# Hybrid attention layer on one core: the last merge's blocks and differences formed in PSUM, output products in another order, softmax sums by a one-operand operation

## The chip, the cores and the metric

The kernel runs on one core of one Trainium2 chip. The core has five queues of work: TensorE (PE in the profile; its weight loads are PEld), VectorE (DVE), ScalarE (ACT), GpSimd (POOL) and SyncE (SP), whose queue here only issues DMA transfers. Two on-chip memories matter: SBUF, from which the matmuls read, and PSUM, eight banks of 128 x 512 floats, into which they write. The metric is the device time of one execution in microseconds (us); lower is better.

## What is computed

One layer over 1024 latent tokens of width 1024, with a prefix of 256 context tokens. An input projection feeds three branches (neighbourhood attention, a short gated convolution, a Conformer convolution); their results are projected, weighted by sigmoid gates and added to m, which goes through one more projection. The parts that the change touches:

```python
def neighbourhood_attention(q, k, v, kc, vc, rpb):
    ...
        s = jnp.concatenate([s_loc.reshape(bsz, n_h, n_cb, Q_COLS, n_loc), s_ctx], axis=-1)
        p = jax.nn.softmax(s, axis=-1).astype(v.dtype)
    ...

def merge_branches(z, ya, yb, yc, w_out_a, w_out_b, w_out_c, w_o):
    ga, gb, gc = jnp.split(jax.nn.sigmoid(z[..., GATES:]), N_BRANCH, axis=-1)
    m = ga * (ya @ w_out_a) + gb * (yb @ w_out_b) + gc * (yc @ w_out_c)
    return m @ w_o

def hybrid_layer(x, xc, c, c_ctx, lp, update_ctx):
    ...
    x = x + gate * merge_branches(z, ya, yb, yc, lp['w_out_a'], lp['w_out_b'], lp['w_out_c'], lp['w_o'])
```

## The kernel before

**Numbers.** All of it is float32. A matrix that goes into a matmul is split in two parts of reduced precision: hi is a cast of it (ACT, L698 in `split`), lo is what the cast leaves (L699, a subtraction on DVE or POOL). Each product is then three matmuls: hi x hi, hi x lo, lo x hi (`mm3`, `product`).

**The attention** (`attend`, `scores`). For two blocks of 128 queries, the scores against context keys (`sc`) and against nearby keys (`sl`) are formed in PSUM; ACT takes the exponentials, and its accumulator gives one sum for the context keys and one for the nearby keys, per block. L571 adds them, L572 takes the reciprocals, L574 multiplies the exponentials; then PE transposes these (L581).

**The merges** (`merge`). m is held transposed: 8 tiles `mt[dm]` of 128 features x 1024 tokens. A merge goes over dm = 0 to 7 and over two halves b of 512 tokens; each half is 12 matmuls into one PSUM bank (`ops`), then L1089 multiplies it by the gates `gs`, loaded from memory, and L1090 adds it to `mt[dm]`. Three merges run one after the other, one per branch: branch 1 first (it writes `mt`, L1087), then branch 0, then branch 2, called the last merge here. In branch 0 L1090 of the first half runs on POOL. Beside branch 0 stand the steps of the Conformer's layer norm (`norm_steps`), which make `ych` and `ycl`, the inputs of the last merge, out of `zcin` (L1178 to L1182 and a split).

**The output product** uses a scheme with seven products for a 2 x 2 block matrix in place of eight. With M11 and M12 the two token halves of dm 0 to 3, and M21 and M22 those of dm 4 to 7, it needs seven right-hand sides, each of four tiles of 128 x 512: M11, M21, M22, MT1 = M12 - M11, MT2 = M22 - MT1, MT3 = M22 - M12 and MT4 = M21 - MT2. Before the change `merge` itself makes M11, MT1 and M21 (`part`); `m_sums(j)` makes the rest behind the merge, from `mt` and three sums `mraw`, all in SBUF. The weights' sums s1 to s4 are made on POOL (`w_sum`, L1257) from rows of w_o that DMA loads into three buffers (`wrf`), and split.

The output has four pairs n of 128-row blocks. `fin_first(n)` computes three products per pair: a1 x M11 into a bank `fa`, which ACT copies to p1 (L1281), s1 x MT1 into `fc`, and then a12 x M21 on top of `fa`; `put` (L1270) multiplies by the residual's gate, adds x and stores by DMA. `fin_rest(n)` has the four others: s2 x MT2 (`ff`), s4 x M22 (`fe`), s3 x MT3 (`fd`), and a22 x MT4 on top of `fd`. L1304 and L1307 combine `ff` with p1 and v.

**What sets the order.** The code names operations in program order; a scheduler then sets the order on each queue by a modelled timeline, and each queue keeps that order. Tile pools set reuse: `ps_x` has six PSUM banks, shared by `ops` and all banks of the output product; `ps_l` has two; `tmp` has six buffers in SBUF. A bank or buffer is written again only after its last reader. `issue_after` keeps `m_sums` behind the copy of p1.

Of the kernel before, what the change touches and what calls it, by code (L numbers as in the profile page):

```python
# [17 lines left out]
P = 128  # L18
# [27 lines left out]
def tile_hybrid(ctx: ExitStack, tc, x, xT, cx, cond, crow, ng, w_ada, b_ada, wqkv, wz,  # L46
# [437 lines left out]
    with tc.tile_pool(name="at", bufs=1, reuse_waits="tile") as at, \  # L484
# [63 lines left out]
        def scores(b0, qd, ql, ks, kc, bias):  # L548
# [8 lines left out]
            for i in range(2):  # L557
# [10 lines left out]
                act.activation(pc, sc[:, i], AF.Exp, bias=mn[:, 2 + i : 3 + i], scale=-1.0, accum_out=mn[:, 4 + i : 5 + i])  # L568
                act.activation(pl, pl, AF.Exp, bias=mn[:, 2 + i : 3 + i], scale=-1.0, accum_out=mn[:, 6 + i : 7 + i])
                pts.append((pt, n))  # L570
            dve.tensor_tensor(out=mn[:, 0:2], in0=mn[:, 4:6], in1=mn[:, 6:8], op=ALU.add)  # L571
# [494 lines left out]
    M11, M21, M22, MT1, MT2, MT3, MT4 = ([None] * 4 for _ in range(7))  # L1066
# [9 lines left out]
    def merge(br, ys, beside=lambda dm, b: None):  # L1076
        for dm in range(KT):
            w = w_merge(br, dm)
            gs = loaded(gd[br * KT + dm], "gs")
            if br == 1:  # L1080
                mt[dm] = of("mt", "mt", F32)
            for b in range(2):
                sl = B512[b]
                ps = ps_x.tile([P, 512], F32, tag="x", name="ops")
                mm3(ps, [(w[k][0], w[k][1], ys[k][0][:, sl], ys[k][1][:, sl]) for k in range(4)])
                if br == 1:
                    dve.tensor_tensor(out=mt[dm][:, sl], in0=ps, in1=gs[:, sl], op=ALU.mult)  # L1087
                else:
                    dve.tensor_tensor(out=gs[:, sl], in0=ps, in1=gs[:, sl], op=ALU.mult)  # L1089
                    (pool if br == 0 and b == 0 else dve).tensor_tensor(out=mt[dm][:, sl], in0=mt[dm][:, sl], in1=gs[:, sl], op=ALU.add)  # L1090
                beside(dm, b)
            if br == 2:
                first, second = halves(mt[dm])
                if dm < 4:
                    part(M11, dm, "ya0", first)
                    sub(dve, first, second, first)
                    part(MT1, dm, "ya1", first)
                else:
                    part(M21, dm - 4, "cv", first)
# [136 lines left out]
    def m_sums(j):  # L1236
        with tc.issue_after(state["fin"].ins):
            t1, b12 = halves(mt[j])
            b21, b22 = halves(mt[4 + j])
            raw = [tmp("mraw") for _ in range(3)]  # L1240
            sub(dve, raw[0], b22, t1)
            sub(dve, raw[1], b22, b12)
            sub(dve, raw[2], b21, raw[0])
            for blocks, t, r in ((MT2, t2, raw[0]), (MT3, t3, raw[1])):
                blocks[j] = t[j]
                split(*t[j], r, dve)
            for blocks, tag, r in ((M22, j, b22), (MT4, 4 + j, raw[2])):
                blocks[j] = halves(hp_pool.tile([P, S], F32R, tag=f"ha{tag}", name="mb"))
                split(*blocks[j], r, dve)
# [43 lines left out]
    def fin_rest(n):  # L1293
# [6 lines left out]
        s2 = w_sum("s2", s1, a11, ALU.subtract)  # L1300
        f = fin_bank("ff")
        product(f, wsplit(s2, pool), MT2, True, True)
        for t in (v, p1):
            dve.tensor_tensor(out=t, in0=f, in1=t, op=ALU.add)  # L1304
        for i, (x_, b, t) in enumerate(((x0, 1, v), (x1, 1, v), (x1, 0, p1))):
            dm = 2 * n + (i > 0)
            dve.scalar_tensor_tensor(out=x_[:, B512[b]], in0=t, scalar=gate[:, dm : dm + 1], in1=x_[:, B512[b]], op0=ALU.mult, op1=ALU.add)  # L1307
        s4 = w_sum("s4", a12, s2, ALU.subtract)
        e = fin_bank("fe")
        product(e, wsplit(s4, dve), M22, True, True)  # L1310
        put(2 * n, 1, e, x0[:, B512[1]])
# [3 lines left out]
        put(2 * n + 1, 1, d, x1[:, B512[1]])  # L1315
        product(d, wsplit(a22, dve), MT4, False, True)
        put(2 * n + 1, 0, d, x1[:, B512[0]])

    t2, t3 = ([halves(of("yb", "mb")) for _ in range(4)] for _ in range(2))
# [3 lines left out]
    for j, ns in enumerate(((0, 1), (2,), (2, 3), (3,))):  # L1323
        m_sums(j)
# [88 lines left out]
```

## Time and profile before

| what | value |
|---|---|
| median of 3 runs | 1121.64 us (1121.34 to 1122.14) |
| profiled execution, its own time | 1122.98 us |
| its span, first to last instruction | 1121.2 us |
| mean granted TensorE clock | 0.989 |
| PE busy 0 to 100 us | 81.24 us |
| PE busy 1000 to 1050 us | 50.00 us |
| PE busy 1050 to 1122 us | 60.83 us |

Times inside the execution are microseconds from the start of the span. A row of a timeline gives start, duration, engine, line, operation, output<-inputs by the program's names and shapes; in brackets the idle time of the engine before it and who ended that. A group of instructions gives count, busy time and mean duration in ns of one, then idle time before them. A stretch of the span gives, behind its length, the busy time and the number of instructions for PE, PEld, DVE, ACT and POOL, then PE's granted clock, the share of DMA and GB/s. PE's durations overlap, since matmuls are pipelined: its pace is read from starts.

### The profile page before, as it was taken

To read this page: it belongs to the slowest core of one execution; us is meant where nothing else is said; L and a number is where in the kernel's file an instruction comes from. 1 tells how busy PE (TensorE), PEld (TensorE's weight loads), DVE (VectorE), ACT (ScalarE), POOL (GpSimd) and SP (SyncE) were. 2 spreads that over 40 slices of the span, in tenths; PEclk is the share of its full clock that TensorE was granted. 3 is DMA by queue.
4 is the path that set the end of the run, shared out by engine and by line. 5 is a ranking of instruction groups with operands and counts; after the bars stand their busy time and mean duration, and the time that the engine had idled before them with its cause. 6 is when DMAs were issued, how large, how long until landed. Compare 5 with 4: busy or idle time off the path is not lost. (4 is left out here: it accounts for less than half of the span.)

```text
span 1121.2 us, 15882 instructions
## 1 busy us (share of the span) xinstructions
PE 1084.2 (97%) x5330; PEld 923.2 (82%) x5330; DVE 832.6 (74%) x1368; ACT 519.8 (46%) x1108; POOL 653.8 (58%) x643
## 2 busy tenths in 40 slices
PE   6889999999999999999999999999999999999998
PEld 5768898998998888887888888888888788878766
DVE  6983478666765655557995997897992479879995
ACT  6764576567556554445233232323434434533430
POOL 2254957437636951104958586868777562783860
PEclk7999999999999999999999999999999999999999
DMA  9555414313312332218133424343436996462443
GB/s 351 203 190 190 122 44 120 94 57 93 118 54 85 122 120 70 67 49 326 38 132 104 151 85 160 103 153 139 129 134 237 408 327 222 140 215 66 126 155 122
DMA packets 79458, 163.17 MB, mean 146 GB/s; under 512 B 10289, under 2 KB 31153, under 8 KB 79281
## 3 DMA queue, kind: packets, MB, share of 16 engines
q1 hardware_dynamic: 74768, 160.06, 41.5%
q10 hardware_dynamic: 4608, 2.10, 0.6%
q8 instruction: 42, 0.69, 0.3%
q14 instruction: 40, 0.32, 0.1%
HBM read 120.18 MB, written 44.50 MB: 147 GB/s over the span
## 5 line engine op out<-in xcount | busy, mean ns | idle before, releaser
L751 DVE SCALAR_TENSOR_TENSOR cv<-upad,cf_t,cv 128x512 f32<-128x512 f32 x240 | 166.8, 744 | 0.1
L699 POOL TENSOR_TENSOR wl<-s,wh 128x512 fp32r<-128x512 f32 x69 | 98.4, 1439 | 21.8 <-ACT wh L698 8.1
L90 POOL TENSOR_TENSOR wl<-wr,wh 128x384 fp32r<-128x384 f32 (+1 forms) x57 | 57.3, 1012 | 68.2 <-ACT wh L88 57.6
L698 ACT CAST wh<-s 128x512 fp32r<-128x512 f32 x92 | 55.9, 616 | 87.6 <-POOL s L702 66.0
L584 DVE TENSOR_TENSOR plo<-pp,phi 128x256 fp32r<-128x256 f32 (+2 forms) x96 | 54.5, 576 | 34.8 <-ACT phi L583 34.4
L541 POOL TENSOR_TENSOR bias<-mk,img 64x96 f32<-64x96 bf16 (+1 forms) x96 | 43.7, 462 | 36.9 <-DVE mn L567 20.5
L699 POOL TENSOR_TENSOR wl<-wr,wh 128x512 fp32r<-128x512 f32 x44 | 60.5, 1375 | 4.2 <-ACT wh L698 4.2
L775 PE MATMUL ga<-ha,wh 128*128 128x512 f32 x152 | 59.3, 390 | 1.2 <-ACT wh L698 1.2
L777 PE MATMUL ga<-ha,wl 128*128 128x512 f32 x152 | 59.2, 390 | 0.0
L776 PE MATMUL ga<-ha,wh 128*128 128x512 f32 x152 | 59.2, 390 | 0.0
L583 ACT CAST phi<-pp 128x256 fp32r<-128x256 f32 (+2 forms) x96 | 46.5, 494 | 26.6 <-PE pp L581 25.9
L567 DVE CUSTOM_DVE_ANT_0 pt<-sl,bias,mn 128x384 f32<-128x384 f32 (+1 forms) x64 | 37.2, 581 | 23.0 <-PE sl L564 21.7
L88 ACT CAST wh<-wr 128x384 fp32r<-128x384 f32 (+1 forms) x66 | 31.6, 487 | 39.8 <-PE zaps L108 14.3
L568 ACT ACTIVATE pt<-sc,mn 128x256 f32<-128x256 f32 x64 | 30.4, 475 | 40.1 <-DVE mn L567 40.0
L581 PE MATMUL pp<-ident,pt 128*128 128x128 f32 x304 | 47.0, 273 | 1.6 <-DVE pt L574 1.6
L803 POOL TENSOR_TENSOR s<-wr 128x512 f32<-128x512 f32 x16 | 23.8, 1486 | 38.7 <-DMA wr<-in_wz 38.6
L581 PEld LDWEIGHTS pp<-ident,pt 128*128 128x128 f32 x304 | 37.4, 140 | 9.0 <-ACT phi L583 1.3
L79 POOL TENSOR_TENSOR ssh<-ssh,half_neg 128x4 f32<-128x4 f32 (+1 forms) x40 | 41.4, 1036 | 2.9
L574 DVE TENSOR_SCALAR pt<-pt,mn 128x640 f32<-128x640 f32 (+1 forms) x64 | 41.6, 692 | 0.9
L78 POOL TENSOR_SCALAR ssh<-ssh 128x4 f32<-128x4 f32 (+1 forms) x40 | 10.5, 261 | 53.1 <-DVE ssh L227 49.4
L964 ACT ACTIVATE c<-c 128x512 f32<-128x512 f32 x18 | 11.4, 633 | 63.6 <-DVE c L781 48.0
L109 PE MATMUL ps<-wh,hb 128*128 128x384 f32 x112 | 39.3, 354 | 1.2 <-DVE hb L353 1.1
(421 smaller groups left out, 3896.8 us busy)
## 6 DMA issues: line engine op xcount, KB each, us to landing
wr<-in_wz SPq DMA_DIRECT2D x34, 512.0 KB, 4.0
gs<-gd SPq DMA_DIRECT2D x24, 512.0 KB, 5.0
wada<-in_w_ada SPq DMA_DIRECT2D x16, 512.0 KB, 8.7
wrf<-in_wo SPq DMA_DIRECT2D x16, 512.0 KB, 3.6
wr<-in_wz SPq DMA_DIRECT2D x36, 192.0 KB, 2.4
cht<-chd SPq DMA_DIRECT2D x24, 256.0 KB, 3.1
wro<-in_wout SPq DMA_DIRECT2D x24, 256.0 KB, 5.2
gd<-gate SPq DMA_DIRECT2D x22, 256.0 KB, 4.2
```

Source lines behind the costliest of these rows:

```text
L90: lo_eng.tensor_tensor(out=lo[:, :n], in0=raw[:, :n], in1=hi[:, :n].bitcast(F32), op=ALU.subtract)
L541: pool.tensor_tensor(out=dst, in0=mv, in1=iv, op=ALU.subtract)
L574: dve.tensor_scalar(out=pt[:, SPAN - n :], in0=pt[:, SPAN - n :], scalar1=mn[:, i : i + 1], scalar2=0.5, op0=ALU.mult, op1=ALU.mult)
L581: pe.transpose(out=pp[:, c * P : c * P + P], in_=src, identity=ident)
L583: act.copy(hi, v)
L584: dve.tensor_tensor(out=lo, in0=v, in1=hi.bitcast(F32), op=ALU.subtract)
L698: act.copy(hi, src)
L699: eng.tensor_tensor(out=lo, in0=src, in1=hi.bitcast(F32), op=ALU.subtract)
L751: dve.scalar_tensor_tensor(out=acc[b], in0=src, scalar=cf_t[:, i, j : j + 1], in1=acc[b], op0=ALU.mult, op1=ALU.add)
L775: pe.matmul(ps, wh, bh, start=first and j == 0, stop=False, skip_group_check=True)
L776: pe.matmul(ps, wh, bl, start=False, stop=False, skip_group_check=True)
L777: pe.matmul(ps, wl, bh, start=False, stop=last and j == 3, skip_group_check=True)
```

## The change

Three edits. The line numbers of the new program are up to 23 higher than those of the old behind the merge.

1. In `scores` the four sums of one step are laid out in pairs, and one `tensor_reduce` over pairs takes the place of the addition of two tensors.
2. In `merge`, L1089 writes its product back into the PSUM bank, and L1090 adds `mt` to it: into `mt` in branch 0, where all of these are now DVE's, and into the bank in the last merge. A new function `blocks` then makes from the banks M11, M21, M22 and MT1 with their splits, and the differences MT2, MT3 and MT4 unsplit (MT2 and MT3 in the two halves of `mt[j]`, MT4 in `t4`); ACT copies a block to SBUF where it is needed as the second operand. `m_sums` gives way to `m_splits`, in which ACT copies each of MT2, MT3 and MT4 into a bank of `ps_l`, from which it is split.
3. In `fin_rest` the product with M22 (`corner`) goes first for pairs 0 to 2; for pair 3 it goes between the two products into `fd`. The sums of `ff` with v and p1 go to PSUM (`fg`, and `ff` itself) and not over p1 and v.

```diff
@@ -565,10 +565,10 @@
                 pt = at.tile([P, SPAN + L], F32, tag="pt", name="pt", bufs=4)
                 pl, pc = pt[:, SPAN - n : SPAN], pt[:, SPAN:]
                 dve.tensor_tensor_reduce(pl, sl[:, :n], bias[:, o : o + n], 1.0, mn[:, i : i + 1], ALU.add, ALU.min, mn[:, 2 + i : 3 + i])
-                act.activation(pc, sc[:, i], AF.Exp, bias=mn[:, 2 + i : 3 + i], scale=-1.0, accum_out=mn[:, 4 + i : 5 + i])
-                act.activation(pl, pl, AF.Exp, bias=mn[:, 2 + i : 3 + i], scale=-1.0, accum_out=mn[:, 6 + i : 7 + i])
+                act.activation(pc, sc[:, i], AF.Exp, bias=mn[:, 2 + i : 3 + i], scale=-1.0, accum_out=mn[:, 4 + 2 * i : 5 + 2 * i])
+                act.activation(pl, pl, AF.Exp, bias=mn[:, 2 + i : 3 + i], scale=-1.0, accum_out=mn[:, 5 + 2 * i : 6 + 2 * i])
                 pts.append((pt, n))
-            dve.tensor_tensor(out=mn[:, 0:2], in0=mn[:, 4:6], in1=mn[:, 6:8], op=ALU.add)
+            dve.tensor_reduce(out=mn[:, 0:2], in_=mn[:, 4:8].rearrange("p (i a) -> p i a", a=2), axis=AX.X, op=ALU.add)
             dve.reciprocal(out=mn[:, 0:2], in_=mn[:, 0:2])
             for i, (pt, n) in enumerate(pts):
                 dve.tensor_scalar(out=pt[:, SPAN - n :], in0=pt[:, SPAN - n :], scalar1=mn[:, i : i + 1], scalar2=0.5, op0=ALU.mult, op1=ALU.mult)
@@ -1063,7 +1063,7 @@
 
 
     mt = [None] * KT
-    M11, M21, M22, MT1, MT2, MT3, MT4 = ([None] * 4 for _ in range(7))
+    M11, M21, M22, MT1, MT2, MT3, MT4, t4 = ([None] * 4 for _ in range(8))
 
     def halves(t):
         return t[:, :512], t[:, 512:]
@@ -1086,17 +1086,38 @@
                 if br == 1:
                     dve.tensor_tensor(out=mt[dm][:, sl], in0=ps, in1=gs[:, sl], op=ALU.mult)
                 else:
-                    dve.tensor_tensor(out=gs[:, sl], in0=ps, in1=gs[:, sl], op=ALU.mult)
-                    (pool if br == 0 and b == 0 else dve).tensor_tensor(out=mt[dm][:, sl], in0=mt[dm][:, sl], in1=gs[:, sl], op=ALU.add)
+                    dve.tensor_tensor(out=ps, in0=ps, in1=gs[:, sl], op=ALU.mult)
+                    dve.tensor_tensor(out=mt[dm][:, sl] if br == 0 else ps, in0=ps, in1=mt[dm][:, sl], op=ALU.add)
+                    if br == 2:
+                        blocks(dm, b, ps)
                 beside(dm, b)
-            if br == 2:
-                first, second = halves(mt[dm])
-                if dm < 4:
-                    part(M11, dm, "ya0", first)
-                    sub(dve, first, second, first)
-                    part(MT1, dm, "ya1", first)
-                else:
-                    part(M21, dm - 4, "cv", first)
+
+    first_half = {}
+
+    def blocks(dm, b, ps):
+
+        j = dm % 4
+        t1, m12 = halves(mt[j])
+        if b == 0:
+            first_half[dm] = ps
+            part((M11, M21)[dm // 4], j, ("ya0", "cv")[dm // 4], ps)
+            if dm < 4:
+                act.copy(t1, ps)
+            return
+        ps0 = first_half[dm]
+        if dm < 4:
+            act.copy(m12, ps)
+            sub(dve, ps0, ps, t1)
+            part(MT1, j, "ya1", ps0)
+            act.copy(t1, ps0)
+        else:
+            M22[j] = halves(hp_pool.tile([P, S], F32R, tag=f"ha{dm}", name="mb"))
+            split(*M22[j], ps, dve)
+            sub(dve, m12, ps, m12)
+            sub(dve, ps, ps, t1)
+            act.copy(t1, ps)
+            t4[j] = tmp("t4")
+            sub(dve, t4[j], ps0, t1)
 
 
 
@@ -1233,20 +1254,14 @@
     merge(2, yc_s)
 
 
-    def m_sums(j):
+    def m_splits(j):
         with tc.issue_after(state["fin"].ins):
-            t1, b12 = halves(mt[j])
-            b21, b22 = halves(mt[4 + j])
-            raw = [tmp("mraw") for _ in range(3)]
-            sub(dve, raw[0], b22, t1)
-            sub(dve, raw[1], b22, b12)
-            sub(dve, raw[2], b21, raw[0])
-            for blocks, t, r in ((MT2, t2, raw[0]), (MT3, t3, raw[1])):
-                blocks[j] = t[j]
-                split(*t[j], r, dve)
-            for blocks, tag, r in ((M22, j, b22), (MT4, 4 + j, raw[2])):
-                blocks[j] = halves(hp_pool.tile([P, S], F32R, tag=f"ha{tag}", name="mb"))
-                split(*blocks[j], r, dve)
+            t2, t3 = halves(mt[j])
+            for blk, src in ((MT2, t2), (MT3, t3), (MT4, t4[j])):
+                blk[j] = halves(hp_pool.tile([P, S], F32R, tag=f"ha{j}", name="mb") if blk is MT4 else of("yb", "mb"))
+                ps = ps_l.tile([P, 512], F32, tag="l", name="copy")
+                act.copy(ps, src)
+                split(*blk[j], ps, dve)
 
     def fin_bank(name):
         return ps_x.tile([P, 512], F32, tag="x", name=name)
@@ -1298,30 +1313,38 @@
         nc.sync.dma_start(x1, xT[2 * n + 1])
         s1 = w_sum("s1", a21, a22, ALU.add)
         s2 = w_sum("s2", s1, a11, ALU.subtract)
+        s4 = w_sum("s4", a12, s2, ALU.subtract)
+
+        def corner():
+            e = fin_bank("fe")
+            product(e, wsplit(s4, dve), M22, True, True)
+            return e
+
+        e = corner() if n < 3 else None
         f = fin_bank("ff")
         product(f, wsplit(s2, pool), MT2, True, True)
-        for t in (v, p1):
-            dve.tensor_tensor(out=t, in0=f, in1=t, op=ALU.add)
-        for i, (x_, b, t) in enumerate(((x0, 1, v), (x1, 1, v), (x1, 0, p1))):
+        g = fin_bank("fg")
+        dve.tensor_tensor(out=g, in0=f, in1=v, op=ALU.add)
+        dve.tensor_tensor(out=f, in0=f, in1=p1, op=ALU.add)
+        for i, (x_, b, t) in enumerate(((x0, 1, g), (x1, 1, g), (x1, 0, f))):
             dm = 2 * n + (i > 0)
             dve.scalar_tensor_tensor(out=x_[:, B512[b]], in0=t, scalar=gate[:, dm : dm + 1], in1=x_[:, B512[b]], op0=ALU.mult, op1=ALU.add)
-        s4 = w_sum("s4", a12, s2, ALU.subtract)
-        e = fin_bank("fe")
-        product(e, wsplit(s4, dve), M22, True, True)
-        put(2 * n, 1, e, x0[:, B512[1]])
+        if e is not None:
+            put(2 * n, 1, e, x0[:, B512[1]])
         s3 = w_sum("s3", a11, a21, ALU.subtract)
         d = fin_bank("fd")
         product(d, wsplit(s3, pool), MT3, True, True)
         put(2 * n + 1, 1, d, x1[:, B512[1]])
+        if e is None:
+            put(2 * n, 1, corner(), x0[:, B512[1]])
         product(d, wsplit(a22, dve), MT4, False, True)
         put(2 * n + 1, 0, d, x1[:, B512[0]])
 
-    t2, t3 = ([halves(of("yb", "mb")) for _ in range(4)] for _ in range(2))
     firsts = [fin_first(n) for n in range(4)]
     for n in (0, 1):
         next(firsts[n])
     for j, ns in enumerate(((0, 1), (2,), (2, 3), (3,))):
-        m_sums(j)
+        m_splits(j)
         for n in ns:
             next(firsts[n], None)
     for n in range(4):
```

The first place is on DVE, at the start of the last merge, where L1090 of its first half stands (`ops` are the PSUM banks, `gs` the gates, `mb` the lo parts of a block). Before:

```order
L1089 TENSOR_TENSOR gs<-ops,gs 128x512 x2
L1090 TENSOR_TENSOR mt<-mt,gs 128x512
L699 TENSOR_TENSOR mb<-mt,mb 128x512
L1089 TENSOR_TENSOR gs<-ops,gs 128x512
L1090 TENSOR_TENSOR mt<-mt,gs 128x512
```

and now:

```order
L1089 TENSOR_TENSOR ops<-ops,gs 128x512 x2
L1090 TENSOR_TENSOR ops<-ops,mt 128x512 x2
L1089 TENSOR_TENSOR ops<-ops,gs 128x512
L699 TENSOR_TENSOR mb<-ops,mb 128x512
L1090 TENSOR_TENSOR ops<-ops,mt 128x512
L699 TENSOR_TENSOR mb<-ops,mb 128x512
L1089 TENSOR_TENSOR ops<-ops,gs 128x512
L702 TENSOR_TENSOR ops<-ops,mt 128x512
```

Every operation now has a bank among its inputs, and a first difference (L702) stands in the middle of the merge; it is the ninth operation from the second L1089 on.

The second place is on ACT, behind the merge, around the copy of the fourth pair's `fa` to p1 (`pv`), on which a product of PE waits (`wh` are casts of weights or of their sums, s2 and s4; `mraw`, `copy` and `t4` belong to the differences). Before:

```order
L698 CAST mb_10509<-mraw_10722 128x512
L698 CAST mb_10513<-mraw_10723 128x512
L698 CAST mb_10732<-mt_9683 128x512
L698 CAST wh_10913<-wrf_10837 128x512
L698 CAST mb_10672<-mraw_10661 128x512
L698 CAST wh_10945<-s2_10942 128x512
L1281 COPY pv_10776<-fa_10759 128x512
```

and now:

```order
L1263 COPY copy_10757<-mt_9358 128x512
L1263 COPY copy_10762<-mt_9358 128x512
L698 CAST mb_10756<-copy_10757 128x512
L698 CAST mb_10761<-copy_10762 128x512
L698 CAST wh_10946<-wrf_10869 128x512
L1263 COPY copy_10767<-t4_10502 128x512
L698 CAST mb_10766<-copy_10767 128x512
L698 CAST wh_10980<-s4_10977 128x512
L1296 COPY pv_10809<-fa_10792 128x512
```

The copy for p1 stood behind a cast of the second pair's s2, and stands now behind one of its s4, which POOL makes two sums later; the casts of `mraw` are casts of banks, each behind a copy.

The third place is on PE, at the end of the last pair's product with MT3, into `fd`. Before:

```order
L775 MATMUL fd_11184<-mb_10514,wh_11185 128x512
L776 MATMUL fd_11184<-mb_10514,wh_11185 128x512
L777 MATMUL fd_11184<-mb_10514,wl_11186 128x512
L775 MATMUL fd_11184<-mb_10622,wh_11204 128x512
L776 MATMUL fd_11184<-mb_10622,wh_11204 128x512
```

and now:

```order
L775 MATMUL fd_11200<-mb_10840,wh_11201 128x512
L776 MATMUL fd_11200<-mb_10840,wh_11201 128x512
L777 MATMUL fd_11200<-mb_10840,wl_11202 128x512
L775 MATMUL fe_11220<-mb_10399,wh_11221 128x512
L776 MATMUL fe_11220<-mb_10399,wh_11221 128x512
```

Where the product with MT4 followed at once on the same bank, 12 matmuls into the bank `fe` now come between.

## The prediction, made before the changed kernel ran

> **What bounds the kernel now.** I read the page's first part, then TensorE's waits, then its rows in order of time where it waits.
>
> ```profile
> PE 1084.2 (97%) x5330; PEld 923.2 (82%) x5330; DVE 832.6 (74%) x1368; ACT 519.8 (46%) x1108; POOL 653.8 (58%) x643
> ```
>
> TensorE (PE) is busy for 97% of the span, so a gain can only come out of the places where it stands still or runs slowly. The change touches the attention (microseconds 127 to 497), the last two merges (936 to 1030) and the output product behind them (to the end). PE's waits from 1000 on:
>
> ```profile
> PE fa L775 <- ACT pv L1281: 2.7, 1, 2.7
> PE fe L776 <- DVE mb L699: 1.9, 1, 1.9
> PE fd L775 <- DVE o L1270: 0.9, 1, 0.9
> ```
>
> The same places as a timeline of PE (start, duration, line, tile; idle time before in brackets):
>
> ```profile
> 984.36 0.39 PE L107 MATMUL ops<-ych,wh 128*128 128x512 f32 x1
> 1029.56 0.39 PE L109 MATMUL ops<-ych,wl 128*128 128x512 f32 x1
> 1059.48 0.39 PE L777 MATMUL fc<-mb,wl 128*128 128x512 f32 x1
> 1062.60 0.50 PE L775 MATMUL fa<-mb,wh 128*128 128x512 f32 x1 [2.73 <-ACT pv L1281]
> ...
> 1080.34 0.57 PE L775 MATMUL ff<-mb,wh 128*128 128x512 f32 x1
> 1112.97 0.39 PE L777 MATMUL fd<-mb,wl 128*128 128x512 f32 x1
> 1114.29 0.47 PE L775 MATMUL fd<-mb,wh 128*128 128x512 f32 x1 [0.94 <-DVE o L1270]
> 1114.60 0.39 PE L776 MATMUL fd<-mb,wh 128*128 128x512 f32 x1
> 1116.87 0.39 PE L777 MATMUL fd<-mb,wl 128*128 128x512 f32 x1
> ```
>
> The last two rows are 10 matmuls apart, so an undisturbed step is 2.27/10 = 0.227 us (the durations overlap). From the first matmul of the last merge (984.36) to the last of all (1116.87) the program has 528: 16 halves x 12, then 28 products x 12. Their 527 steps would take 119.6 us; they take 132.5. **That stage loses 12.9 us**, and this is a ledger of it:
> - (a) 984.36 to 1059.48, 323 steps: 75.1 against 73.3, **1.8** lost. It lies around 993 to 1000.
> - (b) 1059.48 to 1080.34, 49 steps: 20.9 against 11.1, **9.7** lost.
> - (c) 1112.97 to 1114.29, one step: **1.1** lost. The rest, 0.3, is spread.
>
> The waits listed leave some 4 us of (b) open. Two stretches of it, with PE's granted clock behind the busy times:
>
> ```profile
> 1063.00:1067.00 4.00, 4.00 (x12) 3.12 (x11) 4.00 (x6) 0.90 (x2) 0.71 (x1) 0.58 0.98 353
> 1077.00:1081.00 4.00, 4.00 (x13) 3.11 (x12) 4.00 (x5) 1.42 (x3) 3.55 (x3) 0.57 0.61 214
> ```
>
> After the gaps of 2.7 and 1.9 us the clock falls to 0.58 and 0.57 for four microseconds, in which a matmul steps by about 0.43 us. So each gap costs about 1.9 us more (0.20 of every 0.43 in 4 us). [...]
>
> Why the gaps? VectorE (DVE), ScalarE (ACT) and GpSimd (POOL) ahead of the first:
>
> ```profile
> 1055.72 3.48 DVE L699 TENSOR_TENSOR mb<-mraw,mb 128x512 fp32r<-128x512 f32 x2
> 1060.81 1.76 DVE L702 TENSOR_TENSOR mraw<-mt,mraw 128x512 f32<-128x512 f32 x1
> 1065.39 0.68 DVE L699 TENSOR_TENSOR mb<-mt,mb 128x512 fp32r<-128x512 f32 x1
> 1060.92 0.62 ACT L698 CAST mb<-mraw 128x512 fp32r<-128x512 f32 x1 [3.43 <-DVE mb L699]
> 1061.97 0.58 ACT L1281 COPY pv<-fa 128x512 f32<-128x512 f32 x1
> 1060.31 3.41 POOL L699 TENSOR_TENSOR wl<-s,wh 128x512 fp32r<-128x512 f32 x2
> ```
>
> A DVE operation with both inputs in SBUF takes 1.7 us while POOL works and 0.68 us when POOL rests (1065.39). ACT's cast waits 3.43 us for it, and the copy of fa, for which PE waits, is queued behind that cast. DVE's groups from 998 on:
>
> ```profile
> L699 DVE TENSOR_TENSOR mb<-mt,mb 128x512 fp32r<-128x512 f32 x16 | 17.3, 1089 | 0.0
> L699 DVE TENSOR_TENSOR mb<-mraw,mb 128x512 fp32r<-128x512 f32 x12 | 15.7, 1335 | 1.3 <-ACT mb L698 1.2
> L1090 DVE TENSOR_TENSOR mt<-mt,gs 128x512 f32<-128x512 f32 x16 | 14.4, 897 | 0.0
> L1089 DVE TENSOR_TENSOR gs<-ops,gs 128x512 f32<-128x512 f32 x16 | 10.6, 679 | 0.0
> ```
>
> The mean of a group (last number before the bar) tells forms apart: three with two SBUF inputs have 897 to 1335 ns, the one that reads PSUM has 679, POOL or no POOL. DVE is behind: the last L1090 stands at 1036.65, 7 us after the merge's last matmul.
>
> ```profile
> 1036.65 0.69 DVE L1090 TENSOR_TENSOR mt<-mt,gs 128x512 f32<-128x512 f32 x1
> 1014.41 1.28 DVE L699 TENSOR_TENSOR mb<-mt,mb 128x512 fp32r<-128x512 f32 x2
> ```
>
> **The change, part by part.** *Blocks and differences in PSUM.* The count of DVE operations stays: 64 now stand in the merge (16 L1089, 16 L1090, 16 splits, 16 differences) and 12 splits behind it; before there were 48 and 28. What changes is their form: all 76 read one operand from PSUM. Undisturbed, two take 1.28 us (1014.41), a step of 0.60. So the merge's 64 take 64 x 0.60 = 38.4 us, beside 192 x 0.227 = 43.6 us of matmuls; DVE keeps up, with 5 us to spare, and its tail should end some 3 us after the last matmul and not 7. The 12 splits behind take 7.2 us; before, the 12 mb<-mraw alone took 15.7, and 16 more operations stood beside them. Nothing shows a plain two-input operation that writes PSUM; the nearest is the convolution, which accumulates there:
>
> ```profile
> L751 DVE SCALAR_TENSOR_TENSOR cv<-upad,cf_t,cv 128x512 f32<-128x512 f32 x240 | 166.8, 744 | 0.1
> L1270 DVE SCALAR_TENSOR_TENSOR o<-fd,gate,xr 128x512 f32<-128x512 f32 x8 | 6.0, 746 | 8.2 <-PE fd L777 8.2
> ```
>
> PSUM as target (744) costs as much as SBUF (746), beside a busy POOL. Bounds for a step: 0.60, and 0.90 (the mean of mt<-mt,gs) if the target did cost; I take 0.60. [...]
>
> ACT gets 28 more copies (16 in the merge, 12 into PSUM behind it):
>
> ```profile
> L1281 ACT COPY pv<-fa 128x512 f32<-128x512 f32 x4 | 2.3, 580 | 0.0
> 984.00:1081.00 97.00, 90.81 (x378) 72.11 (x377) 88.35 (x100) 34.41 (x61) 65.70 (x42) 0.96 0.42 137
> ```
>
> 28 x 0.58 = 16 us, on an engine busy 34 of these 97: covered. No row has a copy into PSUM; bounds 0.58 and 0.82 (ACT's slowest 512-column form, lsg, further below), and 12 x 0.24 = 3 us more is covered too. I take 0.58. If cover fails, the copy of fa is late again, since it stands behind these copies (rival 1).
>
> A bank is now held until its differences are read, not until L1089. The tightest reuse: the first half of the fourth dm takes the bank of the second half of the first, 72 matmuls after the start, so at 984.4 + 16.3 = 1000.7. That half is complete after 41 matmuls (994), and the DVE order has nine operations from its L1089 to the difference that frees it: 994 + 9 x 0.6 = 999.4. It just fits; as DVE then works off its start, later ones have more room. I keep up to 1 us of loss for it.
>
> *Merge 0.* Eight L1090 go from POOL to DVE:
>
> ```profile
> L1090 POOL TENSOR_TENSOR mt<-mt,gs 128x512 f32<-128x512 f32 x8 | 12.5, 1567 | 14.7 <-PE sums L1116 10.2 <-DVE gs L1089 4.4
> 995.10 2.54 POOL L1182 TENSOR_TENSOR zcin<-zcin,cvin 128x512 f32<-128x512 f32 x2
> 992.24 0.62 ACT L698 CAST ych<-zcin 128x512 fp32r<-128x512 f32 x1 [6.89 <-POOL zcin L1182]
> L1178 ACT ACTIVATE lsg<-cvin,lnb_t,lng_t 128x512 f32<-128x512 f32 x8 | 6.4, 814 | 5.8 <-DVE cvin L1176 3.5 <-POOL cvin L1180 2.3
> ```
>
> The loss (a) comes from POOL: ACT's cast, whose result the last merge multiplies, waits 6.89 us for zcin, and the last zcin ends at 997.6. Five of the eight L1090 stand in POOL's queue between the first zcin and the last, 5 x 1.57 = 8 us, so it should end near 990. But the new order also wants it earlier, 24 to 35 matmuls after the start (990 to 992) and not after 52 (996). I credit 1.0 of the 1.8.
>
> *Behind the merge.* For (b) everything must come early enough. POOL's chain waited for a cast queued behind the blocks of M21, at 1037; these come some 5 us sooner, so POOL's sums for the next pair do too. PE's first fin_rest product becomes the corner, which needs M22, made in the merge, and not MT2. Without stalls it would start at 984.4 + 336 x 0.227 = 1060.6, and MT2's last split, needed at 1065, should be ready near 1057: about 40 ACT instructions stand ahead of it from 1031 on, 40 x 0.58 = 23 us, and a few us of waits. I count 9.2 of the 9.7, clock included.
>
> *Order in the last pair.* The corner now stands between MT3 and MT4 and covers the 0.94 wait for put: 12 x 0.227 = 2.7 us against it. Credit 1.0 of (c)'s 1.1. What follows the last matmul does not change.
>
> *Softmax sums.* 32 small operations:
>
> ```profile
> L571 DVE TENSOR_TENSOR mn<-mn 128x2 f32<-128x2 f32 x32 | 10.2, 318 | 19.7 <-ACT pt L569 19.6
> L574 DVE TENSOR_SCALAR pt<-pt,mn 128x640 f32<-128x640 f32 x48 | 34.1, 738 | 0.7
> L572 DVE RECIPROCAL mn<-mn 128x2 f32<-128x2 f32 x32 | 5.3, 166 | 1.0
> PE pp L581 <- DVE pt L574: 1.6, 2, 1.1
> ```
>
> They take 318 ns where L572, of the same size, takes 166, so some wait for POOL; with one operand 32 x 0.15 = 5 us of DVE go. But PE waits only 1.6 us for what follows, and L574, the multiplication behind, is lengthened by POOL as well and will wait in its stead. Bounds 0 and 1.1; I take 0.3.
>
> **Sum.** 1.0 + 9.2 + 1.0 + 0.3 = 11.5 us. The profiled execution took 1122.98 (span 1121.2 and 1.8 around it), giving 1111.5. The runs shown have a median 1.34 below it; 1121.64 - 11.5 = **1110.1**.
>
> **Rivals.**
> 1. *A gap stays behind the merge.* PE needs the copy of the fourth pair's fa, and in ACT's new order it stands behind three copies into PSUM and the cast of s4, which waits for POOL and POOL for wrf's DMA. For it: that is how the first gap came about. Against: POOL starts earlier. Price: from 1059.48 to the 13th matmul on (1067.03) 7.6 us against 3.0, so 4.6 with its clock; **1114.7**. [...]
> 2. *DVE becomes the bound in the merge*, if a step writing PSUM takes 0.90: 64 x 0.90 = 57.6 against 43.6, and PE, out of banks, waits 14 us and loses 1.9 of clock at least once, against 11.5 gained: +4.4, **1126**. It limits PE from a step of 0.68 on and makes the kernel slower than before from about 0.86. The rows of PSUM forms (679, 744) speak against it.
> 3. *The loss only moves*: the banks held longer stop PE as often as the gaps did. It takes 16 halves x 0.7 us; **1121**. Against: DVE's 5 us of room.
>
> **How the numbers follow.** Forecast 0.62 (1108 to 1113), rival 1 0.24 (1113 to 1118), rival 3 0.07, rival 2 0.07. A range from 1107.5 to 1117 holds the first and most of the second. About 0.2% (2.2 us) is what a measurement of this kernel can tell from no change: faster 0.86, within 0.2% 0.07, slower 0.07.
>
> **What would show it.** In the changed profile: mb<-ops at 0.68 us, no PE wait over 1 us from 1000 on, a clock of 1.0 between 1050 and 1080, the last matmul near 1105.6. It would be wrong if ops<-ops,gs came above 0.75 us, if PE waited for banks around 1001, or if fa still waited for pv.

## The result and the profile after

The changed kernel takes **1108.64 us** (median of 4 runs, 1107.81 to 1109.52), the kernel before beside it 1121.89 (1121.34 to 1123.09). The ratio is 0.9872 with a 95% interval of 0.9858 to 0.9885: faster by 13.25 us. The profiled execution took 1108.79 us, with a span of 1107.0; 1122.98 before, so these two lie 14.19 apart. Two executions, one each of kernels 1 and 7 below, ran at a granted clock of 0.53 and 0.56 and took 2035 and 1803 us; the medians and ratios leave them out.

First the page's busy line, then PE's timeline at the places of the ledger (start, duration, line, tile):

```profile
PE 1076.1 (97%) x5330; PEld 919.6 (83%) x5330; DVE 803.3 (73%) x1376; ACT 534.2 (48%) x1136; POOL 632.8 (57%) x635
```

```profile
983.20 0.39 PE L107 MATMUL ops<-ych,wh 128*128 128x512 f32 x1
...
1026.49 0.39 PE L109 MATMUL ops<-ych,wl 128*128 128x512 f32 x1
...
1056.41 0.39 PE L777 MATMUL fc<-mb,wl 128*128 128x512 f32 x1
1056.64 0.39 PE L775 MATMUL fa<-mb,wh 128*128 128x512 f32 x1
...
1102.68 0.39 PE L777 MATMUL fd<-mb,wl 128*128 128x512 f32 x1
```

The share of PE is 97% as before and says nothing; the starts do. From the first matmul of the last merge to the last of all is called the stage below: 528 matmuls, 132.5 us before, and now 1102.68 - 983.20 = **119.5**, which is 527 undisturbed steps. Every row has 0.39 and none a wait in brackets: the list of PE's waits from 970 on, which had seven entries before, is empty. The merge itself takes 1026.49 - 983.20 = 43.3 us against 1029.56 - 984.36 = 45.2: (a), 1.9. So 13.0 of the 14.2 us are in the stage; the other 1.2 lie ahead of it (983.20 against 984.36).

The span behind the merge, in which the kernel before lost its clock twice, with the granted clock behind the five busy times:

```profile
1050.00:1060.00 10.00, 10.00 (x45) 8.29 (x45) 6.53 (x10) 6.34 (x12) 6.72 (x6) 1.00 0.49 174
1060.00:1070.00 10.00, 10.00 (x45) 8.26 (x45) 4.42 (x7) 1.67 (x3) 6.51 (x5) 1.00 0.68 247
1070.00:1081.00 11.00, 11.00 (x50) 9.12 (x49) 9.15 (x14) 2.49 (x4) 10.82 (x8) 1.00 0.71 211
```

45 matmuls in each 10 us, 50 in the 11, and a clock of 1.00, where the kernel before had 0.58 (1063 to 1067) and 0.57 (1077 to 1081). The groups of DVE from 998 on (mean ns of one before the bar):

```profile
L699 DVE TENSOR_TENSOR mb<-ops,mb 128x512 fp32r<-128x512 f32 x14 | 9.6, 683 | 1.5 <-ACT mb L698 1.4
L1090 DVE TENSOR_TENSOR ops<-ops,mt 128x512 f32<-128x512 f32 x13 | 8.9, 688 | 0.0
L1089 DVE TENSOR_TENSOR ops<-ops,gs 128x512 f32<-128x512 f32 x12 | 8.3, 692 | 1.4 <-PE ops L109 1.3
L699 DVE TENSOR_TENSOR mb<-copy,mb 128x512 fp32r<-128x512 f32 x12 | 8.1, 685 | 7.3 <-ACT mb L698 7.3
...
L702 DVE TENSOR_TENSOR ops<-ops,mt 128x512 f32<-128x512 f32 x7 | 4.8, 688 | 0.0
```

These forms of the change stand at 683 to 692 ns, where the forms with two SBUF inputs had 897 to 1335. And ACT at the copy for which PE waited 2.73 us before, with the cast ahead of it:

```profile
1052.33 0.62 ACT L698 CAST wh<-s 128x512 fp32r<-128x512 f32 x1 [1.85 <-POOL s L1272]
1052.86 0.58 ACT L1296 COPY pv<-fa 128x512 f32<-128x512 f32 x1
```

The copy ends at 1053.4, and PE wants it at 1056.64: 3.2 us in hand. It still stands behind a cast that waits for POOL's sum, as rival 1 had it, but the whole chain runs 9 us earlier (1061.97 before).

### The profile page after: what moved, and what is told of

It reads as the page before. It is cut to its first block, busy times and chain, and to the rows that moved or that the text cites. A ratio compares the mean times of both kernels' runs of the same rounds, so it can differ in the third digit from the quotient of the medians.

```text
span 1107.0 us, 15902 instructions
## 1 busy us (share of the span) xinstructions
PE 1076.1 (97%) x5330; PEld 919.6 (83%) x5330; DVE 803.3 (73%) x1376; ACT 534.2 (48%) x1136; POOL 632.8 (57%) x635
## 4 chain that ended last, share of the span: by engine, by line
PE 75%; DVE 8%; POOL 6%; issue 5%; DMA 2%; ACT 2%; SPq 2%; POOLq 0%; ACTq 0%; DVEq 0%
PE ops L107 4%; PE ops L109 4%; PE ops L108 4%; PE zaps L108 3%; PE zaps L109 3%; PE zaps L107 3%; DVE cv L751 3%; PE py L600 3%; PE pp L581 3%; PE ps L109 3%; PE ps L108 3%; PE ps L107 3%; PE gd L775 2%; PE gd L777 2%; PE gd L776 2%
## 5 line engine op out<-in xcount | busy, mean ns | idle before, releaser
L699 POOL TENSOR_TENSOR wl<-s,wh 128x512 fp32r<-128x512 f32 x69 | 95.2, 1392 | 13.9 <-ACT wh L698 13.1
L90 POOL TENSOR_TENSOR wl<-wr,wh 128x384 fp32r<-128x384 f32 (+1 forms) x57 | 56.8, 1004 | 68.7 <-ACT wh L88 57.9
L699 POOL TENSOR_TENSOR wl<-wro,wh 128x512 fp32r<-128x512 f32 x12 | 17.3, 1445 | 45.1 <-ACT wh L698 45.1
L574 DVE TENSOR_SCALAR pt<-pt,mn 128x640 f32<-128x640 f32 (+1 forms) x64 | 42.3, 702 | 0.9
```

Source lines behind the costliest of these rows:

```text
L90: lo_eng.tensor_tensor(out=lo[:, :n], in0=raw[:, :n], in1=hi[:, :n].bitcast(F32), op=ALU.subtract)
L699: eng.tensor_tensor(out=lo, in0=src, in1=hi.bitcast(F32), op=ALU.subtract)
```

## The experiments

Eleven other kernels, and the changed one once more. Their times are medians; the ratio is to the kernel before on the same chip, comes from all runs kept, and can differ by 0.001 from that of the medians. The stage is read from one profiled execution of each, as above; those of numbers 1, 4 and 7 took 1119.71, 1122.01 and 1122.52 us, which is 1.7 to 2.1 from their medians.

| kernel | us | ratio, 95% interval | stage, us |
|---|---|---|---|
| before | 1121.89 | | 132.5 |
| changed | 1108.64 | 0.9872 (0.9858 to 0.9885) | 119.5 |
| the same again | 1108.43 | 0.9873 (0.9857 to 0.9890) | 119.5 |
| 1 edit 1 alone | 1121.77 | 0.9993 (0.9982 to 1.0004) | 131.8 |
| 2 edit 3 alone | 1123.22 | 1.0011 (1.0002 to 1.0021) | 134.6 |
| 3 edit 2 alone | 1110.75 | 0.9900 (0.9885 to 0.9916) | 120.7 |
| 4 all edits, operands in SBUF | 1119.95 | 0.9974 (0.9961 to 0.9988) | 133.1 |
| 5 before, GpSimd silent | 1113.92 (one run) | | 122.1 |
| 6 changed, eight L1090 on GpSimd | 1116.53 | 0.9942 (0.9924 to 0.9959) | 129.4 |
| 7 before, eight L1090 on DVE | 1124.24 | 1.0021 (1.0010 to 1.0033) | 133.8 |
| 8 changed, no copies into PSUM | 1108.40 | 0.9871 (0.9854 to 0.9888) | 119.5 |
| 9 changed, M22 first in all pairs | 1110.46 | 0.9892 (0.9867 to 0.9916) | 121.1 |
| 10 changed, five banks | 1108.69 | 0.9875 (0.9860 to 0.9890) | 120.4 |
| 11 changed, old softmax sums | 1109.22 | 0.9876 (0.9862 to 0.9891) | 119.9 |

**1 to 3: each edit alone.** Number 1 is the kernel before with the changed lines of `scores`, number 2 with the new `fin_rest`, number 3 the changed kernel with the old `scores` and `fin_rest`.

> The kernel before with edit 1 alone (the sums of the softmax by an operation on one operand). My theory: the softmax gives 0.3 to 0.9 us, at the one wait in the attention near 182 us where the old sum took 1.25 us and that the changed kernel has lost; so 1121.0 to 1121.6 against some 1121.9 of the kernel before, with the stage behind 984 us as it was. Rival: VectorE's shorter queue in the attention also lets later work start earlier and gives 1.5 us or more (below 1120.4). The group at L571 should fall from 318 ns to about 170 if two SBUF operands are what slowed it.

> The kernel before with edit 3 alone (product with M22 first for three pairs and between the two into fd for the last; sums of ff into PSUM); blocks and differences as before, in SBUF. My theory: the gap at the copy of the fourth pair's fa (2.7 us and 1.9 us of clock) comes from slow differences and splits on VectorE and stays; the gap at fe may go or move; the last wait (0.9 and what lies around it, 1.2 us) goes. So 1.2 to 5 us faster than before: 1117 to 1120.7. Rival A: the order alone takes the gaps away, since the first product then needs M22 and not MT2: 1110 to 1112. Rival B: M22 is split behind MT2 and MT3 here, so the new order waits longer: 1122 to 1126.

> The changed kernel with the products' order and the sums of ff as before (edit 2 alone: blocks and differences in PSUM). My theory: (a) and (b) are both gone, since they come from the operands and from GpSimd's relief, and only the last wait stays (1.2 us), and the softmax's 0.3 to 0.9: 1109.5 to 1112. Rival: half or more of (b) comes from the order of the products, since with MT2 first the splits of MT2 (a copy to PSUM, a cast and a difference behind the merge) are late: 1113 to 1118, with a wait of PE for mb near 1060.

Edit 2 alone makes 11 of the 13 us. Edit 3 alone makes the old kernel slower by about 1.2 us (0.2 to 2.4 by its interval), where my theory had it 1.2 to 5 us faster; neither did it free PE (rival A). The longest waits of PE from 930 on in number 2:

```profile
PE fa L775 <- ACT pv L1281: 3.4, 1, 3.4
PE fe L775 <- ACT mb L698: 2.7, 1, 2.7
PE fe L776 <- DVE mb L699: 0.9, 1, 0.9
```

The gap at fa is there as before; the second gap has moved to the product that now comes first: fe waits for the cast of M22, which stands behind MT2 and MT3 in the old `m_sums`, as rival B had it. In number 3 one wait is left:

```profile
PE fd L775 <- DVE o L1285: 0.9, 1, 0.9
```

That is (c). Its stage is 1.2 us longer than that of the changed kernel, so (c) is worth 1.2 with its surroundings, and with (a) at 1.9 the rest of the 13.0, **9.9, is (b), all of it from edit 2**. Number 1 cannot be told from no change, and its median lies just above the 1121.0 to 1121.6 expected; more on it below.

**4: the operands' place apart from the early differences.** The sums and differences stand where the changed kernel has them, but in SBUF; only the splits of M22 stand behind the merge, as in the kernel before:

```diff
-  dve.tensor_tensor(out=ps, in0=ps, in1=gs[:, sl], op=ALU.mult)
-  dve.tensor_tensor(out=mt[dm][:, sl] if br == 0 else ps, in0=ps, in1=mt[dm][:, sl], op=ALU.add)
+  dve.tensor_tensor(out=gs[:, sl], in0=ps, in1=gs[:, sl], op=ALU.mult)
+  dve.tensor_tensor(out=mt[dm][:, sl], in0=mt[dm][:, sl], in1=gs[:, sl], op=ALU.add)
...
-  sub(dve, m12, ps, m12)
-  sub(dve, ps, ps, t1)
...
-  sub(dve, t4[j], ps0, t1)
+  sub(dve, m12, second, m12)
+  sub(dve, t1, second, t1)
...
+  sub(dve, t4[j], first, t1)
```

> The changed kernel with the differences formed at the same places in the merge and the products in the same new order, but every operand of these sums and splits in SBUF: L1089 writes gs, L1090 writes mt, no copies by ScalarE; M22 is split behind the merge, as in the kernel before. My theory: with two operands in SBUF these operations take 0.9 to 1.4 us beside GpSimd and not 0.69, VectorE falls 10 us or more behind, and a gap of PE with a clock drop behind the merge comes back: 5 to 12 us over the changed kernel, 1114 to 1121. Rival: it is the early forming of the differences (spread over the merge rather than heaped behind it) and the order that count, and the operands' place does not: within 1.5 us of the changed kernel, 1107.5 to 1110.

It is some 11 us slower than the changed kernel (a ratio of 0.9974 to the kernel before, against 0.9872); of the whole gain 3 us remain. Its groups of DVE from 998 on and PE's waits from 930 on:

```profile
L699 DVE TENSOR_TENSOR mb<-mt,mb 128x512 fp32r<-128x512 f32 x24 | 26.3, 1111 | 0.2
L1090 DVE TENSOR_TENSOR mt<-mt,gs 128x512 f32<-128x512 f32 x14 | 13.3, 947 | 0.1
L702 DVE TENSOR_TENSOR mt<-mt 128x512 f32<-128x512 f32 x12 | 12.3, 1048 | 0.1
```

```profile
PE fa L775 <- ACT pv L1286: 4.2, 2, 3.4
PE ops L108 <- DVE ycl L699: 3.4, 3, 2.0
```

The same operations take 947 to 1111 ns and not 683 to 692, and the gap at fa is back. The rival, that it is the early forming and the order that count, falls: together they bring 3 us. The start of the merge is worse than before, too: DVE and POOL there, in order of time:

```profile
984.78 1.77 DVE L1090 TENSOR_TENSOR mt<-mt,gs 128x512 f32<-128x512 f32 x1
986.48 1.77 DVE L699 TENSOR_TENSOR ycl<-zcin,ych 128x512 fp32r<-128x512 f32 x1
```

```profile
985.97 1.73 POOL L1192 TENSOR_TENSOR cvin<-cvin,lsg 128x512 f32<-128x512 f32 x1
987.66 1.73 POOL L1194 TENSOR_TENSOR zcin<-zcin,cvin 128x512 f32<-128x512 f32 x1
```

Each engine starts one operation every 1.7 us (984.78 to 986.48, 985.97 to 987.66). With POOL idle, from 992.78 to 995.23, two operations of DVE's form for ycl take 1.28 us:

```profile
993.25 1.28 DVE L699 TENSOR_TENSOR ycl<-zcin,ych 128x512 fp32r<-128x512 f32 x2
```

**5: is it GpSimd?** The kernel before, with GpSimd's work behind the merge left out and nothing else:

```diff
 def w_sum(name, a, b, op):
...
-    pool.tensor_tensor(out=t, in0=a, in1=b, op=op)
-    return t
+    return a
...
-    product(a, wsplit(a11, pool), M11, True, True)
+    product(a, wsplit(a11, None), M11, True, True)
```

(`wsplit` with None casts the high part and uses it for the low one; so in the other products that GpSimd split for.)

> The kernel before, with GpSimd's work for the output product left out: the weights' sums s1 to s4 are not formed (the first operand is taken), and the low part of the weights that GpSimd splits is not formed (the high part is used for it). The differences and splits on VectorE stay, all in SBUF. My theory: what lengthens them is GpSimd; the group mb<-mraw falls from 1335 ns to 0.7 us or less, mb<-mt and mt<-mt,gs to 0.75 us or less behind the first 15 us of the merge, and the gaps of PE behind the merge go: some 1111 us. Rival: their length is that of the form (two operands from SBUF) itself, and stays above 1.0 us with GpSimd silent.

The groups of DVE from 998 on, in the lines of this kernel:

```profile
L1093 DVE TENSOR_TENSOR mt<-mt,gs 128x512 f32<-128x512 f32 x16 | 10.9, 681 | 0.1
...
L699 DVE TENSOR_TENSOR mb<-mt,mb 128x512 fp32r<-128x512 f32 x16 | 10.8, 682 | 0.7 <-ACT mb L698 0.7
...
L699 DVE TENSOR_TENSOR mb<-mraw,mb 128x512 fp32r<-128x512 f32 x12 | 7.9, 686 | 3.4 <-ACT mb L698 3.4
```

With GpSimd silent the same operations with two SBUF inputs take 681 to 686 ns, and the stage loses 122.1 - 119.5 = 2.6 us where it lost 12.9, at (a) and (c) alone: PE has no wait between the merge's start and the last pair. Since this kernel also spares POOL's sums, on which PE's weights depend, the missing gaps alone would not prove the point; the durations do. The time is 2.9 us above the expected 1111: the stage is 10.4 us shorter than that of the kernel before, but starts 1.4 later (985.76 against 984.36), and there is one execution only. What the traces show is the split's mean: with two inputs in SBUF, 686 ns without GpSimd (mb<-mraw) and 1335 beside it in the kernel before, and 685 beside it in the changed kernel with one input in PSUM (mb<-copy).

**6 and 7: the eight L1090 that left GpSimd.** Number 6 puts them back in the changed kernel, number 7 takes them off in the old one.

```diff
 (6)
-  dve.tensor_tensor(out=ps, in0=ps, in1=gs[:, sl], op=ALU.mult)
-  dve.tensor_tensor(out=mt[dm][:, sl] if br == 0 else ps, in0=ps, in1=mt[dm][:, sl], op=ALU.add)
+  on_pool = br == 0 and b == 0
+  dve.tensor_tensor(out=gs[:, sl] if on_pool else ps, in0=ps, in1=gs[:, sl], op=ALU.mult)
+  if on_pool:
+      pool.tensor_tensor(out=mt[dm][:, sl], in0=mt[dm][:, sl], in1=gs[:, sl], op=ALU.add)
+  else:
+      dve.tensor_tensor(out=mt[dm][:, sl] if br == 0 else ps, in0=ps, in1=mt[dm][:, sl], op=ALU.add)
 (7)
-  (pool if br == 0 and b == 0 else dve).tensor_tensor(out=mt[dm][:, sl], ...
+  dve.tensor_tensor(out=mt[dm][:, sl], ...
```

> The changed kernel, in which branch 0's first half is as before: L1089 writes gs, and its eight L1090 run on GpSimd. My theory: (a), the 1.9 us at the start of the last merge, came back from GpSimd's queue, so it is lost again, and nothing else: 1110 to 1111.5, with PE waiting there for ych or ycl. Rival: (a) went because VectorE's and ScalarE's work around the splits of zcin was freed by the operands in PSUM; then this kernel stands within 0.5 us of the changed one, 1108 to 1109.2.

> The kernel before, in which branch 0's first-half L1090 run on VectorE and not on GpSimd, still from SBUF; nothing else changed. My theory, from the kernel whose blocks were formed in SBUF: GpSimd's last zcin ends earlier, but eight additions of up to 1.8 us on VectorE make the splits of zcin late instead, and the start of the last merge loses 1 to 4 us in place of 1.8; the gaps behind the merge stay: 1121 to 1126. Rival, the prediction's own view of (a): GpSimd's relief alone takes 1.0 to 1.9 us of the loss away: 1119.5 to 1121.

Number 6 missed its expectation by 5 us, to the worse. PE loses 8.9 us at one place, where it waits for a bank and then runs at a lower clock (a wait of 0.7 at fd adds 0.8):

```profile
997.62 0.39 PE L109 MATMUL ops<-ych,wl 128*128 128x512 f32 x1
1004.07 0.80 PE L107 MATMUL ops<-ych,wh 128*128 128x512 f32 x1 [6.07 <-DVE ops L702]
```

```profile
1004.00:1008.00 4.00, 3.93 (x9) 3.14 (x10) 3.35 (x7) 3.55 (x7) 0.00 (x0) 0.50 0.43 135
```

DVE starts the merge's first product with the gates (L1089, which is L1090 in number 6) at 994.87 and the first difference at 1003.33; in the changed kernel these stand at 991.47 and 996.85. POOL's last zcin comes ahead of them:

```profile
990.13 2.53 POOL L1207 TENSOR_TENSOR zcin<-zcin,cvin 128x512 f32<-128x512 f32 x2
...
994.87 1.38 DVE L1090 TENSOR_TENSOR ops<-ops,gs 128x512 f32<-128x512 f32 x2
...
1003.33 1.28 DVE L702 TENSOR_TENSOR ops<-ops,mt 128x512 f32<-128x512 f32 x2
```

```profile
991.47 1.29 DVE L1089 TENSOR_TENSOR ops<-ops,gs 128x512 f32<-128x512 f32 x2
992.67 1.28 DVE L1090 TENSOR_TENSOR ops<-ops,mt 128x512 f32<-128x512 f32 x2
...
996.85 0.69 DVE L702 TENSOR_TENSOR ops<-ops,mt 128x512 f32<-128x512 f32 x1
```

So 3.4 us come from POOL's late zcin (it ends at 992.66, in the changed kernel at 990.18, and two splits of zcin follow it in place of one), and 3.1 from the order that the scheduler then gave DVE (more products and additions ahead of the difference). PE wants the bank 72 matmuls after the start: in the changed kernel at 983.20 + 16.3 = 999.5, where it comes free at 997.5. Number 7 loses at the same place from the other side: its stage loses 4.0 us more than the kernel before within the first 68 matmuls, waiting three times for ycl (the longest wait 1.95, with a clock of 0.57 from 994 to 998), whose splits DVE does late: it is busy for 7.96 of the 8 us from 986 to 994, and the additions that now stand between the splits take up to 1.78 us in number 4, where they run on DVE from SBUF too. So taking the eight off GpSimd is worth nothing by itself (slower by 0.2%), and forming the blocks in PSUM without it loses 8 us again, more than half of the gain; only together do they make (a) go.

**8 to 10: three smaller parts.** Number 8 drops the copy into PSUM of `m_splits`, number 9 has `e = corner()` for every pair, number 10 gives `ps_x` five banks.

```diff
 (8)
-  ps = ps_l.tile([P, 512], F32, tag="l", name="copy")
-  act.copy(ps, src)
-  split(*blk[j], ps, dve)
+  split(*blk[j], src, dve)
 (9)
-  e = corner() if n < 3 else None
+  e = corner()
 (10)
-  ps_x = ctx.enter_context(tc.tile_pool(name="ps_x", bufs=6, space=PSUM, reuse_waits="tile"))
+  ps_x = ctx.enter_context(tc.tile_pool(name="ps_x", bufs=5, space=PSUM, reuse_waits="tile"))
```

> The changed kernel without ScalarE's 12 copies into PSUM behind the merge: MT2, MT3 and MT4 are split straight from SBUF. My theory: the heap of two-SBUF-operand work behind the merge is now small (12 splits at 1.1 to 1.4 us and not 28 operations), and VectorE has 7 us of idle time there, so nothing or a little is lost: 1108 to 1110.5. Rival: it is these splits beside GpSimd that made the gap, and it comes back with its clock drop: 1112 to 1116, with PE waiting for pv or mb between 1055 and 1075.

> The changed kernel with the product with M22 first in the last pair too, so that MT4 follows MT3 on one bank at the end as before. My theory: the wait for the store's operation on VectorE comes back, 0.9 us and 1.2 with what lies around it: 1109.5 to 1110.2. Rival: the wait is hidden otherwise, 1108.2 to 1109.0.

> The changed kernel with five PSUM banks in place of six for the merges and the output product. My theory: at the start of the last merge a bank is freed some 3 us before it is wanted (the first L702 at 996.85, the product that takes a bank at about 1000); with one bank less the next half asks 12 matmuls, 2.7 us, sooner, so PE waits there for 0 to 3 us, and a clock drop of up to 2.8 us may follow; behind the start VectorE is faster than PE and the banks come in time: 1109 to 1115. Rival: five banks are too few all through the merge, each half waits, and it is 1118 or more.

The 12 copies are not needed. Without them 8 of the splits take twice as long, beside a DVE that has time for it:

```profile
L699 DVE TENSOR_TENSOR mb<-mt,mb 128x512 fp32r<-128x512 f32 x8 | 10.8, 1382 | 2.7 <-ACT mb L698 2.7
```

and the stage stays at 119.5. Number 9 brings (c) back (a wait of 0.9 at fd, the stage 1.6 longer); its median is 0.3 above the range expected. Number 10 has one wait of 0.7 for a bank at the start of the merge, no clock drop behind it (1.00 from 996 to 1004), and its time, 0.3 below the range expected, cannot be told from that of the changed kernel: six banks have a little to spare, five just do.

**11: the softmax's sums.** The changed kernel without edit 1, and the changed kernel once more beside it.

> The changed kernel without edit 1 (the softmax's sums as before). My theory: the wait of PE for L574 near 182 us comes back (1.5 us in place of 0.2), and 0.7 to 1.3 us are lost, since behind the attention no gap of PE is left that could give it back: 1109.3 to 1110. Rival: it is hidden here too, 1108.4 to 1108.9.

> The changed kernel itself once more, beside the one with the old softmax sums on the same chip: 1107.8 to 1109.5, as before.

The medians are 1109.22, just below the 1109.3 to 1110 expected, and 1108.43, as expected; but their runs overlap (1107.21 to 1110.16, 1108.03 to 1108.89), so the time alone doesn't settle it. The trace shows the place. The operation at L571 in the kernel before, and in the changed one (shortest, median, longest duration in ns):

```profile
L571 DVE TENSOR_TENSOR mn<-mn x32: 148/161/1247, 137.4 to 495.3; 128x2 f32<-128x2 f32 x32
```

```profile
L571 DVE TENSOR_REDUCE mn<-mn x32: 140/156/159, 136.7 to 493.7; 128x2 f32<-128x4 f32 x32
```

The mean of 318 ns was a median of 161 and a few long ones. In the kernel before eight of them last over 250 ns, and each ends within 0.04 us of the end of an operation of GpSimd that had begun before it. GpSimd's operation (to 181.31) and the longest sum on DVE (to 181.33):

```profile
179.70 1.61 POOL L649 TENSOR_TENSOR hsum<-hb 128x512 f32<-128x512 f32 x1
...
180.08 1.25 DVE L571 TENSOR_TENSOR mn<-mn 128x2 f32<-128x2 f32 x1
```

L574 comes late behind it, and PE's matmul at 184.47 waits 1.13 us for L574. In PE's waits of 100 to 500 the entry pp <- pt is 1.7 us with the old sums (number 11), 0.2 in the changed kernel:

```profile
PE pp L581 <- DVE pt L574: 1.7, 3, 1.1
```

```profile
PE pp L581 <- DVE pt L574: 0.2, 1, 0.2
```

Number 11's matmuls fall 1.0 us behind the other's between the 870th and the 900th. In number 1 the same place was gained, 0.7 us, but the gaps behind the merge are waits for things that had their own time: the first grew from 2.73 to 3.66 us.

## Why the prediction was right, and where its terms were off

The forecast was 1110.1 us with a range of 1107.5 to 1117, and it is 1108.64: the main path came as told, and the terms were a little too small. (The ledger's "some 4 us of (b) open" takes in two waits at ff, of 0.5 and 0.3 us, that its list of waits leaves out without a mark; by the waits that it shows, 5.1 are open.)

- **DVE's step in the merge: right.** 0.60 us was taken, with 0.90 as the other end; two L1089 from 991.47 on take 1.29 us and the next group starts 1.20 behind them, a step of 0.60, and the forms that write PSUM take 688 to 692 ns, against 679 for the old L1089, which wrote SBUF. That rules rival 2 out. The tail is not as told: the last L1090 stands at 1028.44, 2 us behind the last matmul, but the last differences wait for ACT and end at 1034.4. Nothing wanted them sooner.
- **ACT's copies: right.** 0.58 was taken, between 0.58 and 0.82. Into PSUM they take 594 to 603 ns:

```profile
L1263 ACT COPY copy<-mt 128x512 f32<-128x512 f32 x8 | 4.5, 594 | 0.0
L1263 ACT COPY copy<-t 128x512 f32<-128x512 f32 x4 | 2.4, 603 | 1.1 <-DVE mb L699 1.1
```

- **The banks: right, by little.** Up to 1 us was kept for the tightest reuse, and it cost nothing. Rival 3's wait is what number 6 shows, 8.9 us at one place.
- **(a), credit 1.0: 1.9 came.** That POOL's last zcin would end near 990 was right (988.44 + 1.74):

```profile
988.44 1.74 POOL L1203 TENSOR_TENSOR zcin<-zcin,cvin 128x512 f32<-128x512 f32 x1
```

  But the reason given, GpSimd's relief, is half of it. By number 7, DVE's additions from SBUF would have cost more than the relief brings; they had to read PSUM.
- **(b), credit 9.2: 9.9 came.** The mechanism (two SBUF inputs beside GpSimd make DVE late, DVE makes ACT late, ACT the copy of fa) is shown by numbers 3, 4 and 5, with the waits in the trace before. The part that the order of products was given in it, that the first product needs M22 and not MT2, is not: number 3 has the old order and no gap.
- **(c), credit 1.0: 1.2 came**, by numbers 3 and 9.
- **Softmax, 0.3 taken between 0 and 1.1: 0.7 to 1.0 came**, by the traces of number 1 (0.7), of the kernels before and after (0.9) and of number 11 (1.0). L574 does take longer beside POOL: two take 2.29 us at 194.17 in the kernel before, with POOL busy, and 1.02 at 204.61, with POOL idle. The step that was mis-sized is that it "will wait in its stead": PE's wait for L574 shrank from 1.7 to 0.2 us, since no late L571 stands ahead of it.
- **Rival 1** had the right place. The copy still stands behind a cast that waits for POOL, and 3.2 us keep it off PE's path.

The credits add up to 11.5, the profiled executions differ by 14.2: the 2.7 between them are 0.9 of (a), 0.7 of (b), 0.2 of (c), 0.6 of the softmax, and 0.3 elsewhere ahead of the stage, for which no run shows a cause. The medians differ by 13.25.

## What to carry to other kernels

Look at the duration of one form beside a busy neighbour and beside a resting one before counting operations: here a subtraction cost 0.68 or 1.3 us by where its operands lay, and moving them into PSUM, with the count unchanged, was worth some 11 of the 13 us (numbers 3 and 4). An engine that is not the bottleneck can still set the pace through a chain of three queues, and here it showed in the idle time of the engine in the middle (ACT's 3.43 us). Parts of a change can need each other: number 7 was slower alone, and without it number 6 lost 8 of the 13 us.

## What the runs showed of the hardware that was not expected

In these runs the clock drop behind a gap does not go by the gap's length. The kernel before fell to 0.58 and 0.57 behind gaps of 2.73 and 1.94 us; number 7 has gaps of 1.66, 2.15 and 1.94 at the same places and keeps its clock (1.00 from 1056 to 1084), though earlier in the same execution it lost it behind 1.95:

```profile
993.78 0.58 PE L108 MATMUL ops<-ycl,wh 128*128 128x512 f32 x1 [1.95 <-DVE ycl L699]
...
1070.98 0.50 PE L775 MATMUL ff<-mb,wh 128*128 128x512 f32 x1 [2.15 <-ACT mb L698]
...
1077.21 0.50 PE L776 MATMUL fe<-mb,wh 128*128 128x512 f32 x1 [1.94 <-DVE mb L699]
```

```profile
994.00:998.00 4.00, 4.00 (x11) 3.10 (x11) 2.94 (x6) 0.26 (x1) 1.27 (x1) 0.57 0.87 296
1072.00:1076.00 4.00, 2.98 (x12) 1.80 (x10) 4.00 (x5) 1.01 (x2) 3.92 (x3) 1.00 0.01 2
1076.00:1080.00 4.00, 2.79 (x12) 2.31 (x13) 4.00 (x4) 1.14 (x2) 4.00 (x4) 1.00 0.21 76
```

Number 1 even kept 1.00 behind 3.66 us and lost it behind 2.18:

```profile
1062.00:1066.00 4.00, 4.00 (x18) 3.00 (x16) 4.00 (x7) 1.14 (x2) 0.09 (x1) 1.00 0.93 343
1070.00:1074.00 4.00, 3.53 (x10) 2.43 (x8) 4.00 (x3) 0.24 (x1) 3.92 (x4) 0.64 0.00 0
```

What decides is open. The 1.9 us that the prediction laid on each gap was thus the price in that one execution. A price that changes from execution to execution may also be why 27 runs of the kernel before on one chip spread over 5.4 us (1120.46 to 1125.89), and the changed kernel, without gaps, in eight runs over 1.7 (1107.81 to 1109.52); no run here tests that apart.

A tiny operation waited for a long one: adding two columns of 128 numbers to two others, 161 ns by its median, took up to 1247, to the end of GpSimd's operation, and its sibling on one operand, in 32 instances, never more than 159.
